# Decode attention over compressed blocks in the row layout of the other decode branches, with one sum tile for all three

## The chip, the cores and the metric

One Trainium2 chip, one core. The metric is the device time of one execution in microseconds; the time before is the median of three runs. TensorE (PE) does the matrix products and loads its weights in a queue of its own (PEld); VectorE (DVE) and ScalarE (ACT) do element-wise work and move results out of PSUM; GpSimd (POOL) and SyncE (SP) mainly start transfers.

## The reference, cut to what matters

One layer of a decoder: a prompt of 256 tokens and 8 single decode tokens, each with 2048 cached tokens. Two mixers run on the same normed input, sparse attention and a gated DeltaNet. Their outputs are gated, projected, merged and added to the residual. The change touches only the decode side of the sparse attention. It has three branches for each of 8 sequences: attention over compressed blocks (127 for each sequence, 32 tokens each, made by a small two-layer network), over selected blocks, and over a window of 512. Eight query heads in 2 groups of 4 share 2 key/value heads. The attention weights over the compressed blocks also choose the selected blocks.

```python
kc, vc = compress_finish(jnp.concatenate([pk_past, pk_new], axis=1),
                         jnp.concatenate([pv_past, pv_new], axis=1), cw)   # kc is RMS-normed
o_cmp, p_cmp = cmp_attend(q, kc, vc, qpos, slopes)                         # scores - slope * distance
idx, valid = select_blocks(p_cmp, qpos, kc.shape[1], -(-(past_len + DS) // SEL_BLOCK))
o_slc = slc_sample(q, kv_slc, cache_slc, page_table, idx, valid, qpos, past_len, slopes)
...
o = g[:, :, 0] * o_cmp + g[:, :, 1] * o_slc + g[:, :, 2] * o_win           # g: sigmoid gates per head
```

## The kernel before

The backbone is a list `halves` of weight pieces. Each piece is loaded by SP into `raw` (three buffers), split into a rounded part `hi` by ScalarE (L332, L409) and a residual `lo` by VectorE (L333, L410), three buffers each, and used by TensorE in three products (`three`, L316) that add up in one of two PSUM banks `acc`. First come the compressions of the 8 sequences' cached keys and then values (`CQ`, 96 products for each sequence, `acc<-hi,w1h` and the like), then the projections of the layer, then the output projections. Between the halves `tick()` advances generators (L253) that trace everything else; `yield n` lets n ticks pass. A scheduler orders the instructions of TensorE, VectorE and ScalarE by priority and by when operands and buffers are free; SP and POOL keep the written order. Tiles of one tag share their buffers: `s8` has 13 large slots, `a` has 5 buffers of up to 264 columns (`NA`, L207), `psb` and `psl` have two PSUM banks each. The input norm `g_xnorm` (L279) runs during the compression of the keys; its sums go over long VectorE reduces (L295) and up to four `a` tiles at once (L300, L301).

The decode attention is in these generators:

- `g_cmp_fin` (L437), for each sequence: activation, the second layer of the network into `kcT` or `vc`, squares `csq` in an `a` buffer, and their sums over 128 channels by two products with a column of ones (L468), copied into `rkc` (L469), whose inverse root is taken once at the end (L472).
- `g_small` (L603): the gates. `gd` holds the compressed branch's gates for 64 query columns, `grow` those of the other two branches by row.
- `g_dec_cmp` (L647): scores as 127 blocks x 64 columns. Each sequence's keys meet all 64 query columns, and `diag` (L641) picks the 4 columns that belong to the sequence. Then a transpose, softmax over 64 rows, a transpose back, the value products with all 64 columns (L680), again `diag`, the gates, and the block scores (`dci`) from which the selection follows.
- `g_dec_slc` (L882) and `g_dec_win` (L812): the other two use a row layout instead. Query columns sit in a tile `qm` with zeros, `qk` (L787) makes four 32-column products side by side, one for each pair of group and sequence parity, and softmax runs over 128 rows of which 64 are used. Values go through `pv_part` (L801) into `po`, and `pv_take` (L808) copies them by ScalarE into a tile `X` for each branch.
- at the end of `g_dec_win` (L870) a gather `smo` adds both `X` tiles (2 x 8 products of 8 columns) and the new token's part to `oD`; after it `g_oa` (L1579) frees `oA`, and `g_gdn` starts with `dec` (L1140).

Of the kernel before, what the change touches and what calls it, by code (L numbers as in the profile page):

```python
# [20 lines left out]
NB = 8  # L21
# [34 lines left out]
def shape_constants():  # L56
# [19 lines left out]
    sl64 = np.broadcast_to(slope.reshape(2, 1, 4), (2, NB, 4)).reshape(64)  # L76
    c.add("cmpb", -(PAST - kendd)[:, None] * sl64[None])
# [67 lines left out]
def program(tc, A):  # L145
# [26 lines left out]
    def psb(name):  # L172
        return ps_s.tile([128, 512], F32, tag="ps", name=name)
# [55 lines left out]
    rkc = cp.tile([128, 16], F32, name="rkc")  # L229
# [9 lines left out]
    gd = cp.tile([128, 64], F32, name="gd")  # L239
    grow = cp.tile([128, 2], F32, name="grow")  # L240
# [196 lines left out]
    def g_cmp_fin(kv, b, ps, n):  # L437
# [10 lines left out]
        if kv == 0:  # L448
# [9 lines left out]
            p3 = psb("cf")  # L458
            if b is None:
                for g in range(2):  # L460
                    mm(p3[:, 16 * g:16 * g + 15], ones, sq[:, g, :nn])
# [39 lines left out]
    def g_qstat(h):  # L501
# [7 lines left out]
        if h == 7:  # L509
# [19 lines left out]
            qx = slot("qm", [128, 640])  # L529
            G.memset(qx, 0.0)  # L530
# [72 lines left out]
    def g_small(ps):  # L603
# [24 lines left out]
        mm(p2[:, 0:64], ones[0:24, :], x[:, 0:2].rearrange("p a b r -> p (a b r)"))  # L628
        S.activation(gd, p2[:, 0:64], AF.Copy)
        xp = tp.tile([24, 2, 2, 2, 32], F32, name="gxp", tag="a", bufs=NA)  # L630
        V.memset(xp, 0.0)
        for br in range(2):
            for c in range(2):
                V.tensor_copy(xp[:, br, c, :, 0:16].rearrange("p g (i r) -> p g i r", r=4),
                              x[:, 2 + 2 * br:4 + 2 * br].rearrange("p a (i c) r -> p c a i r", c=2)[:, c])
            mm(p2[:, 192 + br:193 + br], xp[:, br].rearrange("p c g x -> p (c g x)"), ones[0:24, 0:1])
        V.tensor_copy(grow, p2[:, 192:194])
        V.tensor_scalar(beh, smt[:, :, 64:72], 0.5, None, ALU.mult)
        mark("small")

# [1101 lines left out]
```

## Time and profile before

| | |
|---|---|
| median of three runs | 1137.02 us (1135.52 to 1137.14) |
| the profiled execution | 1137.88 us, span 1136.2 us |
| mean granted TensorE clock | 0.994 |
| TensorE busy | 1112.4 us, 98% |
| VectorE busy | 697.1 us, 61% |
| ScalarE busy | 572.7 us, 50% |
| DMA | 222.17 MB, mean 196 GB/s |

The page's chain of work that ended last is 92% TensorE. A timeline row gives start, duration, engine, line, operation, output tile <- inputs, shape and count; a merged row covers all its instructions, and in brackets stands the idle time before it with its cause. A matmul on 32-bit floats shows as two instructions. Durations of matmuls overlap, so the distance between two starts tells more than a duration does.

### The profile page before, as it was taken

The numbers are of one execution on the slowest core, as the hardware profiler recorded it, in microseconds if no ns is written. First come the engines' busy times: TensorE is split into PE (matmuls) and PEld (weight loads), VectorE is DVE, ScalarE is ACT, GpSimd is POOL, SyncE is SP. The second block draws the span as 40 slices with busy tenths as digits, with TensorE's granted clock in tenths as the row PEclk, the third lists the DMA queues.
The fourth block names the chain that finished last, engine by engine and source line by source line (L and its number), as shares of the span: only waits on it lengthen the run. The fifth ranks groups of instructions, "written<-read, shape, count | busy, mean of one in ns | idle before, by whom it ended". The sixth has DMA issues, their size and how long they took to land.

```text
span 1136.2 us, 25323 instructions
## 1 busy us (share of the span) xinstructions
PE 1112.4 (98%) x9558; PEld 1069.3 (94%) x9558; DVE 697.1 (61%) x1523; ACT 572.7 (50%) x1138; POOL 144.2 (13%) x227
## 2 busy tenths in 40 slices
PE   4999999999999999999999999999999999999998
PEld 3989999999999987897989999999999999999998
DVE  3578565443657776783566577677547575487443
ACT  4445655444634766673454465545344554444332
POOL 4430244200001310113022100102000000000000
PEclk9989999999999999999999899999999999999999
DMA  9873676435445784568998755657454355556663
GB/s 302 255 241 124 202 205 203 152 95 160 161 138 177 218 214 135 159 196 220 281 390 291 268 174 176 201 179 220 138 187 148 119 165 177 181 184 223 201 236 125
DMA packets 77069, 222.17 MB, mean 196 GB/s; under 512 B 10625, under 2 KB 27850, under 8 KB 75410
## 3 DMA queue, kind: packets, MB, share of 16 engines
q1 hardware_dynamic: 59346, 164.36, 44.7%
q0 software_dynamic: 15008, 44.98, 13.8%
q10 hardware_dynamic: 2592, 11.21, 2.6%
q8 instruction: 75, 1.23, 0.4%
q14 instruction: 48, 0.39, 0.1%
HBM read 202.90 MB, written 17.60 MB: 194 GB/s over the span
## 4 chain that ended last, share of the span: by engine, by line
PE 92%; DVE 1%; ACT 0%; issue 0%; ACTq 0%
PE acc L205 77%; PE inv L205 1%; PE po L205 1%; PE gtr L202 1%; PE pvo L205 1%; PE ps L205 1%; PE gsc L205 1%; PE cf L205 1%; PE kk L205 1%; PE vnb L202 1%; PE uw L205 1%; DVE xt L306 1%; PE pst L202 0%; PE og L205 0%; PE wsc L205 0%; PE kvtr L202 0%
## 5 line engine op out<-in xcount | busy, mean ns | idle before, releaser
L333 DVE TENSOR_TENSOR lo<-raw,hi 128x1024 fp32r<-128x1024 f32 (+1 forms) x250 | 304.8, 1220 | 212.5 <-ACT hi L332 206.1
L205 PE MATMUL acc<-xh,hi 128*128 128x264 f32 (+1 forms) x1488 | 433.8, 292 | 0.0
L332 ACT ACTIVATE hi<-raw 128x1024 fp32r<-128x1024 f32 (+1 forms) x250 | 263.9, 1056 | 329.7 <-PE acc L205 269.0
L205 PE MATMUL acc<-xl,hi 128*128 128x264 f32 (+1 forms) x1488 | 426.9, 287 | 0.5 <-issue 0.5
L205 PE MATMUL acc<-xh,lo 128*128 128x264 f32 (+1 forms) x1488 | 426.3, 287 | 0.0
L205 PEld LDWEIGHTS acc<-xh,hi 128*128 128x128 f32 (+1 forms) x1488 | 281.0, 189 | 7.6 <-issue 7.0
L205 PEld LDWEIGHTS acc<-xh,lo 128*128 128x128 f32 (+1 forms) x1488 | 280.0, 188 | 2.7 <-issue 2.2
L205 PEld LDWEIGHTS acc<-xl,hi 128*128 128x128 f32 (+1 forms) x1488 | 281.1, 189 | 1.5 <-issue 1.0
L205 PE MATMUL acc<-hi,w1h 128*128 128x254 f32 (+1 forms) x512 | 148.1, 290 | 15.9 <-ACT hi L409 15.9
L205 PE MATMUL acc<-lo,w1h 128*128 128x254 f32 (+1 forms) x512 | 147.4, 288 | 3.4 <-DVE lo L410 3.2
L205 PE MATMUL acc<-hi,w1l 128*128 128x254 f32 (+1 forms) x512 | 145.7, 285 | 0.0
L410 DVE TENSOR_TENSOR lo<-rawc,hi 128x512 fp32r<-128x512 f32 (+2 forms) x136 | 84.0, 656 | 52.5 <-ACT hi L409 48.1
L205 PEld LDWEIGHTS acc<-hi,w1h 128*128 128x128 f32 x512 | 98.4, 192 | 16.0 <-ACT hi L409 15.9
L409 ACT ACTIVATE hi<-rawc 128x512 fp32r<-128x512 f32 (+2 forms) x136 | 74.7, 599 | 62.7 <-PE acc L205 58.0
L205 PEld LDWEIGHTS acc<-lo,w1h 128*128 128x128 f32 x512 | 99.2, 194 | 4.8 <-DVE lo L410 4.5
L205 PEld LDWEIGHTS acc<-hi,w1l 128*128 128x128 f32 x512 | 99.0, 193 | 0.1
L386 POOL DMA_DIRECT2D rawc<-ccmp x125 | 67.3, 538 | 98.2 <-issue 72.3
L205 PE MATMUL acc<-oh,hi 128*128 128x264 f32 x256 | 73.5, 287 | 0.0
L205 PE MATMUL acc<-oh,lo 128*128 128x264 f32 x256 | 72.9, 285 | 0.0
L205 PE MATMUL acc<-ol,hi 128*128 128x264 f32 x256 | 72.7, 284 | 0.0
L205 PE MATMUL acc<-mh,hi 128*128 128x264 f32 x256 | 72.6, 284 | 0.0
L205 PE MATMUL acc<-ml,hi 128*128 128x264 f32 x256 | 72.5, 283 | 0.0
(452 smaller groups left out, 1476.4 us busy)
## 6 DMA issues: line engine op xcount, KB each, us to landing
raw<-win SPq DMA_DIRECT2D x184, 512.0 KB, 3.5
raw<-wpab SPq DMA_DIRECT2D x32, 512.0 KB, 3.9
raw<-wo SPq DMA_DIRECT2D x32, 512.0 KB, 4.3
rawc<-ccmp SPq DMA_DIRECT2D x126, 128.0 KB, 2.7
rawc<-ccmp POOLq DMA_DIRECT2D x125, 128.0 KB, 3.3
raw<-w SPq DMA_DIRECT2D x8, 512.0 KB, 7.6
wk<-winK SPq DMA_DIRECT2D x8, 512.0 KB, 11.1
o_wk<-wk POOLq DMA_DIRECT2D x8, 512.0 KB, 9.0
```

What stands on the lines that cost most here:

```text
L202: T.transpose(out, in_, ident[0:n, 0:n])
L205: T.matmul(out, lhsT, rhs, start=start, stop=stop, **k)
L306: V.scalar_tensor_tensor(xt[i][:, k, :], xt[i][:, k, :], P("nw")[:, kk:kk + 1], rx, ALU.mult, ALU.mult)
L332: S.activation(self.hi, self.raw, AF.Copy)
L333: V.tensor_sub(self.lo, self.raw, self.hi)
L386: e.dma_start(rawc[kv, b][j // 8][:, j % 8].rearrange("p s c g -> p (s c g)"), src[kv, bass.ds(r, 1)].rearrange("o d f -> (o d) f"))
L409: S.activation(h, src, AF.Copy)
L410: V.tensor_sub(l, src, h)
```

## The change

The compressed branch takes the row layout: `qk` makes the scores as 128 rows x 127 blocks, and the softmax runs on them in place. The inverse key norms are needed by row, so the squares of two sequences are summed by four 32-column products with a 0/1 matrix `four` into a PSUM tile `css` that lives from sequence 1 to 7; an even sequence's `csq` waits for the odd one. The weights are transposed once ungated (for the block scores, read from PSUM) and once gated, and the value products are 32-column tiles over key rows 0 to 63 and 64 to 126. Their result is copied into one tile `X`, which lies in the slot of `qm`; the other two branches add theirs by VectorE. The gather reads one `X`. `g_small` makes three row gates. `diag`, `gd`, `rkc` and the two old `X` slots go.

```diff
-    c.add("cmpb", -(PAST - kendd)[:, None] * sl64[None])
+    c.add("kd", np.broadcast_to(-(PAST - kendd)[None], (128, NCMP)))
+    c.add("four", np.broadcast_to((np.arange(60) // 4 == 7)[None], (128, 60)))
...
+            elif b % 2 == 0:
+                L["csq"] = sq
             else:
-                for g in range(2):
-                    mm(p3[0:127, g:g + 1], sq[:, g, :], ones[:, 0:1])
-                V.tensor_copy(rkc.rearrange("p (g b) -> p g b", g=2)[0:127, :, b], p3[0:127, 0:2])
-                if b == NB - 1:
-                    rk = tp.tile([128, 16], F32, name="rk2", tag="rk2")
-                    rsq(rk[0:127], rkc[0:127], 1.0 / 128, 4 * EPS, [127, 16])
-                    V.tensor_scalar(rkc[0:127], rk[0:127], SCALE, None, ALU.mult)
+                if b == 1:
+                    L["css"] = psl("css")
+                i, sqs = b // 2, (L.pop("csq"), sq)
+                for j in range(4):
+                    mm(L["css"][32 * j:32 * j + 32, 0:127], C("four")[:, 28 - 4 * i:60 - 4 * i], sqs[j // 2][:, j % 2, :],
+                       start=i == 0, stop=i == 3)
+                if i == 3:
+                    rsq(rkr, L.pop("css")[:, 0:127], 1.0 / 128, 4 * EPS, [128, 127])
+                    V.tensor_scalar(rkr, rkr, SCALE, None, ALU.mult)
...
-            qx = slot("qm", [128, 640])
-            G.memset(qx, 0.0)
+            qx = slot("qm", [128, 1664])
+            G.memset(qx[:, 0:640], 0.0)
+            L["X"] = qx[:, 640:1664].rearrange("p (b d) -> p b d", b=NB)
...
-        mm(p2[:, 0:64], ones[0:24, :], x[:, 0:2].rearrange("p a b r -> p (a b r)"))
-        S.activation(gd, p2[:, 0:64], AF.Copy)
...
-        for br in range(2):
+        for br in range(3):
+            xp = tp.tile([24, 2, 2, 32], F32, name="gxp", tag="a", bufs=NA)
+            V.memset(xp, 0.0)
...
+            mm(p2[:, br:br + 1], xp.rearrange("p c g x -> p (c g x)"), ones[0:24, 0:1])
...
-        for g in range(2):
-            pt = psb("dcs")
-            for b in range(NB):
-                mm(pt[0:127, 64 * b:64 * b + 64], L["kcT"][:, b, g, :], qf)
-            for o, pv, w in diag(pt[0:127], SCm[0:127], g):
-                V.tensor_tensor(o, pv, rkc[0:127, 8 * g + w.start:8 * g + w.stop, None].to_broadcast([127, w.stop - w.start, 4]),
-                                ALU.mult)
-        V.tensor_add(SCm[0:127], SCm[0:127], C("cmpb", 127))
+        SC = tp.tile([128, 127], F32, name="dcs", tag="a", bufs=NA)
+        PT = tp.tile([128, 128], F32, name="dcp", tag="a", bufs=NA)
+        m1 = tp.tile([128, 4], F32, name="dcm", tag="dcm")
+        pt = psb("dcs")
+        for i in range(4):
+            qk(pt, i, lambda c, g: L["kcT"][:, 2 * i + c, g, :])
+        V.tensor_mul(SC, pt[:, 0:127], rkr)
+        V.scalar_tensor_tensor(SC, C("kd"), C("c64")[:, 1:2], SC, ALU.mult, ALU.add)
...
         yield 5
-        p2 = psb("dct")
-        tr(p2[0:64, 0:127], SCm[0:127, :])
...
         p3 = psb("dct")
-        tr(p3[0:127, 0:64], E[:, 0:127])
-        V.tensor_copy(PT[0:127], p3[0:127, 0:64])
+        tr(p3[0:127, 0:128], SC)
...
+        V.tensor_scalar(SC, SC, grow[:, 0:1], None, ALU.mult)
         yield 3
-        for g in range(2):
-            p5 = psb("dcv")
-            for b in range(NB):
-                mm(p5[:, 64 * b:64 * b + 64], L["vc"][0:127, b, g, :], PT[0:127, :])
-            for (o, pv, _), (_, gv, _) in zip(diag(p5, oD, g), diag(p5, oD, g)):
-                V.tensor_copy(o, pv)
-        V.tensor_mul(oD, oD, gd)
+        tr(p3[0:127, 128:256], SC)
+        S.activation(PT[0:127], p3[0:127, 128:256], AF.Copy)
...
+        yield 2
+        for b in range(NB):
+            if b % 4 == 0:
+                po = PV("pvo")
+            for g in range(2):
+                for t, rows in enumerate((slice(0, 64), slice(64, 127))):
+                    j, c, o = 2 * g + t, 2 * (b % 2) + g, 128 * (b % 4)
+                    mm(po[32 * j:32 * j + 32, o:o + 128], PT[rows, 32 * c:32 * c + 32], L["vc"][rows, b, g, :])
+            if b % 4 == 3:
+                S.activation(L["X"][:, b - 3:b + 1, :], po.rearrange("p (b d) -> p b d", b=4), AF.Copy)
...
-    def pv_take(po, w, b):
+    def pv_take(po, b):
         if b % 4 == 3:
-            S.activation(L["X", w][:, b - 3:b + 1, :], po.rearrange("p (b d) -> p b d", b=4), AF.Copy)
+            x = L["X"][:, b - 3:b + 1, :]
+            V.tensor_add(x, x, po.rearrange("p (b d) -> p b d", b=4))
...
-        for w in range(2):
-            for b in range(NB):
-                mm(o[:, :, b, :], L["X", w][:, b, :], gx[:, :, b, :], start=False, stop=w * b == 7)
-        V.tensor_add(oD, oD, pt[:, 0:64])
-        del L["X", 0], L["X", 1]
+        for b in range(NB):
+            mm(o[:, :, b, :], L["X"][:, b, :], gx[:, :, b, :], start=False, stop=b == 7)
+        V.tensor_copy(oD, pt[:, 0:64])
```

## Rows read from the trace of the kernel before

**Rows 1.** Busy times of the page: us, share of the span, instructions.

```profile
PE 1112.4 (98%) x9558; PEld 1069.3 (94%) x9558; DVE 697.1 (61%) x1523; ACT 572.7 (50%) x1138; POOL 144.2 (13%) x227
```

**Rows 2.** What TensorE waited for: us in total, times, longest us.

```profile
PE acc L205 <- ACT hi L409: 15.9, 1, 15.9
PE acc L205 <- DVE lo L410: 3.2, 2, 2.6
```

**Rows 3.** Stretches of 20 us: busy us of each engine, clock, DMA share, GB/s.

```profile
60.00:80.00 20.00, 17.44 (x121) 16.99 (x120) 15.43 (x18) 9.34 (x16) 6.98 (x13) 0.83 0.83 256
80.00:100.00 20.00, 19.90 (x166) 19.45 (x166) 19.32 (x39) 13.34 (x21) 1.07 (x2) 1.00 0.15 40
```

**Rows 4.** TensorE's timeline around one isolated sum of squares (start, duration).

```profile
142.92 0.50 PE L205 MATMUL cf<-cst,csq 128*127 128x1 f32 x4
143.28 0.38 PE L205 MATMUL acc<-lo,w1h 128*128 128x286 f32 x1
143.50 0.29 PE L205 MATMUL acc<-hi,w1l 128*128 128x286 f32 x1
143.62 0.30 PE L205 MATMUL acc<-hi,w1h 128*128 128x286 f32 x1
```

**Rows 5.** TensorE's timeline at the first of the two groups of scores.

```profile
315.21 1.88 PE L205 MATMUL dcs<-qd,kcT 128*127 128x64 f32 x16
316.90 0.36 PE L205 MATMUL acc<-xh,lo 128*128 128x264 f32 x1
```

**Rows 6.** TensorE's timeline at the value products of the compressed branch.

```profile
334.53 3.68 PE L205 MATMUL dcv<-dcp,vc 127*128 127x64 f32 x32
338.02 0.37 PE L205 MATMUL acc<-xl,hi 128*128 128x264 f32 x1
```

**Rows 7.** TensorE's timeline at the gather and what follows it.

```profile
630.90 1.46 PE L205 MATMUL smo<-cst,X 128*128 128x8 f32 x12
632.21 0.42 PE L202 MATMUL cvt<-cst,qkvr 128*128 128x128 f32 x2
632.47 2.30 PE L205 MATMUL smo<-cst,X 128*128 128x8 f32 x20
634.62 1.36 PE L205 MATMUL dec<-smt,cst 128*128 128x8 f32 x8
635.83 0.57 PE L205 MATMUL acc<-xh,hi 128*128 128x264 f32 x1
```

**Rows 8.** Two stretches after the gather, columns as in rows 3.

```profile
634.00:635.90 1.90, 1.90 (x16) 1.90 (x15) 0.19 (x1) 0.00 (x0) 0.00 (x0) 0.80 1.04 433
635.90:641.90 6.00, 6.00 (x28) 6.00 (x28) 1.90 (x7) 1.49 (x3) 0.00 (x0) 0.50 0.99 335
```

**Rows 9.** TensorE's timeline at 32-column products of the DeltaNet's decode.

```profile
660.86 1.08 PE L205 MATMUL sw<-sst,wq 128*32 128x128 f32 x32
661.87 0.39 PE L205 MATMUL acc<-xl,hi 128*128 128x264 f32 x1
662.10 0.28 PE L205 MATMUL acc<-xh,lo 128*128 128x264 f32 x1
```

**Rows 10.** TensorE's timeline at products in tiles of 32 rows and columns.

```profile
812.62 0.44 PE L205 MATMUL inv<-P,prod 32*32 32x16 f32 x32
812.99 1.10 PE L205 MATMUL inv<-U,At 128*128 128x64 f32 x8
```

**Rows 11.** VectorE's timeline between 60 and 92 us.

```profile
60.87 0.16 DVE L469 COPY rkc<-cf 127x2 f32<-127x2 f32 x1 [1.21 <-PE cf L205]
...
71.27 1.26 DVE L410 TENSOR_TENSOR lo<-rawc,hi 128x512 fp32r<-128x512 f32 x2
...
91.26 0.43 DVE L444 SCALAR_TENSOR_TENSOR chs<-ct,cy 128x254 f32<-128x254 f32 x1
```

**Rows 12.** ScalarE's timeline: the squares of the third sequence.

```profile
68.11 0.36 ACT L456 ACTIVATE csq<-cf 128x254 f32<-128x254 f32 x1
```

More of the change, by code (lines that the diff above doesn't have):

```diff
@@ L228, in program @@
     hb = cp.tile([128, 2], F32, name="hb")
-    rkc = cp.tile([128, 16], F32, name="rkc")
+    rkr = cp.tile([128, NCMP], F32, name="rkr")
     kcTp = cp.tile([128, 2, 15], F32, name="kcTp")
@@ L238, in program @@
     smt = cp.tile([128, 2, 72], F32, name="smt")
-    gd = cp.tile([128, 64], F32, name="gd")
-    grow = cp.tile([128, 2], F32, name="grow")
+    grow = cp.tile([128, 3], F32, name="grow")
     acc2 = cp.tile([128, 128], F32, name="acc2")
@@ L457, in g_cmp_fin @@
             yield 8
-            p3 = psb("cf")
             if b is None:
+                p3 = psb("cf")
                 for g in range(2):
@@ L627, in g_small @@
         p2 = psb("gdp")
[L628 to L632 removed]
+        for br in range(3):
+            xp = tp.tile([24, 2, 2, 32], F32, name="gxp", tag="a", bufs=NA)
+            V.memset(xp, 0.0)
             for c in range(2):
[L634 to L637, printed above, removed]
+                V.tensor_copy(xp[:, c, :, 0:16].rearrange("p g (i r) -> p g i r", r=4),
+                              x[:, 2 * br:2 * br + 2].rearrange("p a (i c) r -> p c a i r", c=2)[:, c])
+            mm(p2[:, br:br + 1], xp.rearrange("p c g x -> p (c g x)"), ones[0:24, 0:1])
+        V.tensor_copy(grow, p2[:, 0:3])
         V.tensor_scalar(beh, smt[:, :, 64:72], 0.5, None, ALU.mult)
         mark("small")
[L641 to L644 removed]
     def g_dec_cmp():
@@ L671, in g_dec_cmp @@
+        V.reciprocal(m1[:, 2:3], m1[:, 1:2])
+        V.tensor_scalar(SC, SC, m1[:, 2:3], None, ALU.mult)
+        yield 5
         p3 = psb("dct")
-        tr(p3[0:127, 0:64], E[:, 0:127])
-        V.tensor_copy(PT[0:127], p3[0:127, 0:64])
+        tr(p3[0:127, 0:128], SC)
         PR = tp.tile([128, 16], F32, name="dpr", tag="dpr")
-        V.tensor_reduce(PR[0:127], PT[0:127].rearrange("p (c r) -> p c r", r=4), AX.X, ALU.add)
-        yield 3
-        for g in range(2):
-            p5 = psb("dcv")
-            for b in range(NB):
-                mm(p5[:, 64 * b:64 * b + 64], L["vc"][0:127, b, g, :], PT[0:127, :])
-            for (o, pv, _), (_, gv, _) in zip(diag(p5, oD, g), diag(p5, oD, g)):
-                V.tensor_copy(o, pv)
@@ L683, in g_dec_cmp @@
-        V.tensor_mul(oD, oD, gd)
+        for c in range(2):
+            V.tensor_reduce(PR[0:127].rearrange("p (g i c) -> p c g i", g=2, c=2)[:, c],
+                            p3[0:127, 64 * c:64 * c + 64].rearrange("p (g x) -> p g x", g=2)[:, :, 0:16]
+                            .rearrange("p g (i r) -> p g i r", r=4), AX.X, ALU.add)
+        V.tensor_scalar(SC, SC, grow[:, 0:1], None, ALU.mult)
+        yield 3
+        tr(p3[0:127, 128:256], SC)
+        S.activation(PT[0:127], p3[0:127, 128:256], AF.Copy)
@@ L773, in row_softmax @@
         V.reciprocal(sn[:, 3:4], sn[:, 3:4])
-        V.tensor_mul(sn[:, 3:4], sn[:, 3:4], grow[:, w:w + 1])
+        V.tensor_mul(sn[:, 3:4], sn[:, 3:4], grow[:, w + 1:w + 2])
         V.tensor_mul(sn[:, 4:5], sn[:, 4:5], sn[:, 3:4])
@@ L1580, in g_oa @@
         yield from wait("attn")
-        yield from wait("oD", 2)
+        yield from wait("oD")
         for g in range(2):
```

23 lines of the change are left out of this document (4 added, 19 removed).

## The prediction

> **What bounds the kernel now.** I read the page's busy times first. TensorE is busy for 1112.4 of 1136.2 us, VectorE for 61% of the span [rows 1]. Next comes the list of what TensorE waited for. One wait of 15.9 us for the first cache pages lies at the start, waits for the residual split (`lo`, VectorE) come to 3.2 us, and nearly nothing else is there [rows 2]. So the time is the sum of what TensorE has in its queue, and an instruction taken out of that queue is worth its start-to-start spacing. It isn't worth its listed duration, because matmuls overlap: in the plain stream one `acc` matmul starts 0.12 us after the other and lists 0.29 [rows 4]. Everything below is counted in spacings. [...] Around 70 us TensorE waits for VectorE, and its clock is low for part of that stretch (0.83 over 60 to 80 us) [rows 2, 3]. [...]
>
> **What is removed, all on the path.** (1) The squares of the compressed keys are summed by two matmuls with one moving column for each of 8 sequences, and each shows as two instructions. An isolated group of four starts at 142.92, `acc` goes on at 143.28, and the first `acc` after it takes 0.22 instead of 0.12 to its successor [rows 4]: 0.36 + 0.10 = 0.46 us. Eight groups: 3.7 us. (2) The scores of all 64 query columns against every sequence's keys: two groups of 16 instructions, 1.69 us from the first to the next `acc` [rows 5], with some 0.1 for the change over: 2 x 1.75 = 3.5 us. (3) The value products, 32 instructions from 334.53 to 338.02 [rows 6], with the change over 3.6 us. (4) Half of the final gather, because there is one sum tile instead of two: 12 instructions took 1.31 us and 20 took 2.15 [rows 7], that is 0.108 each; 16 of them are 1.7 us. Together 12.5 us.
>
> **What is added.** The replacement for (1) to (3) uses weights of 32 columns, so four products lie side by side in the array. The trace has just this form: 32 instructions `sw`, 128 rows by 32 columns with 128 moving columns, from 660.86 to 661.87, 0.0316 us each, and the next `acc` is 0.10 late [rows 9]. I count 0.10 ahead of a group as well, so 0.20 for each group. Key squares: now once for two sequences, 4 groups of 8, each 8 x 0.0316 + 0.20 = 0.45, together 1.8 us. Scores: 32 x 0.0316 + 0.20 = 1.2 us. Value products: 64 instructions, since each key range is cut into rows 0 to 63 and 64 to 126; 64 x 0.0316 + 0.20 = 2.2 us. Together 5.2 us. Bounds: the shortest row of tiles that differ in rows and columns is `inv`, 32 instructions in 0.37 us [rows 10], 0.012 each, though with 16 moving columns; with that for the value products and with no change over for the squares, 3.1 us. At the other end short groups may not overlap (0.09 for each instruction of the squares, from rows 4: 2.9 + 0.8 us) and the value products may take twice the spacing (4.2): 9.1 us. I take 5.2, because `sw` has the same shape.
>
> [...] In rows 10, tiles on different rows write one PSUM tile at 0.012 us each, so they do overlap. [...]
>
> **Edits that I cost at nothing on the path.** The gate tile now gets three columns by 3 matmuls (6 instructions) where 1 + 2 stood (6 as well). The two transposes stay two. VectorE loses 8 copies of two columns and gets a reciprocal root over 127 columns instead of 16, 12 operations and a scaling: each is under the 0.63 us that a 512-column subtraction costs [rows 11], so at most 8 us spread around 160 us. VectorE has the room there; TensorE shows no wait after 80 us except some tenths [rows 2]. The four sum-tile adds move from ScalarE to VectorE, again about 0.63 us each, four in 90 us. What is queued behind such an add is the next `lo`; three `raw`, `hi` and `lo` buffers stand between it and TensorE. If that cover were gone, each add would cost its 0.63 us, 2.5 us together. No DMA and no work on the SP or POOL queue is moved past another, except that the constants grow by 123 columns (63 KB) and that two 8 KB slots fewer are taken late in the kernel, which can only let loads go earlier.
>
> **What is not passed on.** The first two groups of squares lie ahead of the wait at 70 us, which ends when `lo` does [rows 11]. What TensorE saves before (0.46 x 2 - 0.45 = 0.5 us) only lets it wait longer. VectorE loses one copy there that had waited 1.21 us for TensorE [rows 11]; at most 1.4 us could come back, but the long reduce behind the copy hangs on ScalarE too, and I count 0.2. That leaves 0.3 us to take off.
>
> **The sum.** 12.5 - 5.2 - 0.3 = 7.0 us. The profiled execution took 1137.88 us (span 1136.2), so it would take 1130.9; the median of the three runs is 0.9 below it, 1137.0, and with that the forecast is 1130.0 us. With the two bounds of the added work: 3.1 to 9.1 us, that is 1134 to 1128.
>
> **The rivals.** *The clock stays up.* From 630.7 to 635.8 TensorE runs only matmuls of 8 columns (two `cvt` of 128 between them), and in this stretch the clock falls: the last 8 take 1.21 instead of 0.86 us and the next 28 `acc` take 6.0 instead of 3.4 [rows 7, 8]. That is 3.0 us. The change cuts the stretch to about 3.4 us. For a clock that stays: the value products, 3.5 us of 64-column matmuls, passed with the clock at full [rows 6]. Against: around 70 us a wait of only 2.6 us was enough for a fall [rows 2, 3], and 8 columns are nearer to a wait than to 64. The time would be 1127. [...]
>
> *Buffers run short, and it ends slower.* The squares of an even sequence now stay in one of the five `a` buffers until the odd one is done. Those written at 68.11 [rows 12] would stay until about 96 us, while the input norm keeps up to four `a` tiles between 78 and 96 us and the next sequence needs three; `chs` at 91.26 [rows 11] then comes some 6 us later, and the evacuation of an accumulator may wait too. It happens where VectorE is busy for 19.3 of 20 us [rows 3]. The accumulators have two banks, so it costs nothing until the delay is longer than one sequence's 96 matmuls, 11.5 us; beyond that TensorE stands still for each further microsecond, and a stop of over 2 us brings a half-clock stretch of about 3 us as at 70 us. For a result slower than before the stops must come to over 7 us. Two such stops of 4 us with 3 us of low clock each give 14 - 7, about 1144. Against it: the tiles of the norm are gone by 97 us, and so is the shortage.
>
> *The tiles don't pack.* If 32-column products start at 0.11 us like the ones they replace, 128 instructions cost 14.1 us, with change overs 15.3, where 10.8 are taken away, and the 1.7 of the gather is all that stands against it: 1139.8. Rows 9 speak against it for just this shape.
>
> *The wait at 70 us goes too.* If the order on VectorE shifts so that `lo` comes ahead of the long reduce, 2.6 us and the low clock behind it (about 3 us) come back: 1124.
>
> **How the numbers follow.** Forecast 0.52; clock stays up 0.25; buffers run short 0.09, about half of it with no more than a loss of part of the gain; tiles don't pack 0.05; the wait goes 0.09. Likeliest: 1130.0 us. The range reaches down past the clock case, to 1125.5, and up to the upper bound of the added work, 1134.5; outside lie the wait that goes (0.09), the tiles that don't pack and most of the shortage, less than 0.2. About 0.2% (2.3 us) is what a measurement of this kernel can tell from no change. Faster: forecast, clock, wait and part of the shortage, less the tail above 1134.7, 0.86. Same: 0.08, from the shortage and the upper bound. Slower: 0.06.
>
> **What would show it.** In the changed profile: 32 score instructions in about 1 us, 64 value instructions in about 2 us and contiguous, 16 gather instructions in 1.7 us, groups of 8 squares in 0.25 us; TensorE's busy time lower by about 7 us with its idle time as before, and the clock near 630 us either at half for some 7 us again (forecast) or at full. Wrong would be: value products at 0.06 or more, a new wait of TensorE for an `acc` bank or for `lo` between 80 and 170 us, or a TensorE that is idle for more than 26 us.

## The result and the profile after

The change makes the kernel slower. In six runs each it takes 1144.37 us (median; 1142.61 to 1147.28) where the kernel before takes 1135.78 (1134.74 to 1137.14): ratio 1.0075, 95% interval 1.0059 to 1.0091. The forecast was 1130.0 with a range of 1125.5 to 1134.5. The profiled execution took 1142.61 us (span 1140.7, mean granted clock 0.992). It is the fastest of the six, and the kernel before was profiled above its median (1137.88 us), so the two traces lie 4.7 us apart and not 8.6.

TensorE's work shrank, by less than the 7 us of the forecast. This is the busy line of the page after, which answers to [rows 1]:

```profile
PE 1107.1 (97%) x9574; PEld 1062.2 (93%) x9574; DVE 699.8 (61%) x1516; ACT 573.5 (50%) x1136; POOL 145.6 (13%) x227
```

TensorE is busy 5.3 us less and the span is 4.5 us longer, so its idle time grew by 9.8 us. The list of what it waited for, kernel after (us in total, times, longest), which answers to [rows 2], says where:

```profile
PE acc L205 <- ACT hi L408: 15.8, 2, 14.5
PE pvo L205 <- DMA wv<-winV: 3.2, 3, 1.8
PE acc L205 <- DVE lo L409: 3.0, 2, 1.9
PE pvo L205 <- DMA gv<-cslv,idx: 2.3, 1, 2.3
PE rrow L202 <- DVE aT L1176: 1.5, 1, 1.5
PE dq L205 <- DVE dkq L1414: 1.4, 1, 1.4
PE kk L205 <- DVE edl L1162: 1.0, 1, 1.0
PE uw L205 <- ACT wT L1292: 0.7, 1, 0.7
PE kk L205 <- DVE l L1158: 0.7, 1, 0.7
PE acc L205 <- ACT gate L1498: 0.6, 1, 0.6
```

The first and third line are old. The others are new, and none of them names an instruction that the change wrote: selected values (`gv`), window values (`wv`), the DeltaNet's chain (`rrow`, `kk`, `dq`), a gate. But for `uw` (at 884 us) they fall in four stretches (kernel after; busy us of PE, PEld, DVE, ACT, POOL with their counts, clock, DMA share, GB/s):

```profile
540.00:550.00 10.00, 7.73 (x73) 7.12 (x72) 1.53 (x4) 1.69 (x2) 0.00 (x0) 0.83 1.03 287
600.00:620.00 20.00, 16.83 (x176) 15.06 (x174) 10.80 (x17) 8.43 (x17) 4.51 (x8) 0.95 0.90 336
640.00:660.00 20.00, 17.96 (x152) 16.58 (x152) 14.86 (x42) 13.73 (x33) 0.00 (x0) 0.91 0.42 138
700.00:710.00 10.00, 6.90 (x64) 5.77 (x56) 7.40 (x25) 8.58 (x28) 0.00 (x0) 0.84 0.52 179
```

Each of them has idle time and a mean clock under 1. The trace's clock record has the granted clock at 0.50 for 3.4 us from 546.5, 6.8 us from 618.1, 3.4 us from 648.8 and 3.4 us from 706.9 us. Two of these begin within a wait, the others 0.7 and 1.4 us behind the end of one. At 0.50 one `acc` starts 0.22 us after the other, at 1.00 it is 0.12. So a wait with such a stretch behind it costs its own length, and then about half the length of the stretch.

The changed parts themselves, on TensorE's timeline of the kernel after (start, duration, instructions): a quarter of a group of squares (two of its eight instructions), the scores, the value products, the gather. They answer to [rows 4 to 7].

```profile
143.30 0.29 PE L205 MATMUL acc<-hi,w1l 128*128 128x286 f32 x1
143.52 0.41 PE L205 MATMUL css<-csq,cst 128*32 128x127 f32 x2
143.85 0.52 PE L205 MATMUL acc<-hi,w1h 128*128 128x286 f32 x2
...
312.59 1.08 PE L205 MATMUL dcs<-kcT,qm 128*32 128x127 f32 x32
313.60 0.39 PE L205 MATMUL acc<-xh,lo 128*128 128x264 f32 x1
...
334.61 1.95 PE L205 MATMUL pvo<-vc,dcp 64*32 64x128 f32 x64
336.49 0.39 PE L205 MATMUL acc<-xh,hi 128*128 128x264 f32 x1
...
633.14 1.90 PE L205 MATMUL smo<-cst,qm 128*128 128x8 f32 x16
634.90 1.04 PE L205 MATMUL dec<-smt,cst 128*128 128x8 f32 x8
635.79 0.37 PE L205 MATMUL acc<-xh,hi 128*128 128x264 f32 x1
```

The scores take 1.01 us from first to next `acc`, the value products 1.88 (0.029 each), the 16 gather instructions 1.76 (0.11 each). Behind the gather, where the kernel before ran at half clock [rows 8], the kernel after has:

```profile
632.00:634.90 2.90, 2.90 (x29) 2.90 (x27) 0.95 (x1) 1.38 (x3) 0.00 (x0) 1.00 0.86 218
634.90:641.90 7.00, 7.00 (x61) 7.00 (x61) 4.50 (x15) 2.35 (x6) 0.00 (x0) 1.00 0.69 227
```

To place gain and loss I compare the start of the same dense product (the n-th `acc` matmul; their order is the same in all kernels) in two traces. The table gives that difference to the kernel before, at times of the kernel before, less its value at 195 us. That point is taken because kernels whose first 300 us are the same instructions still differ by up to 4.5 us by then. Negative is ahead. It is one execution each, so tenths mean little, but steps of 2 us can be placed.

| kernel | 500 | 590 | 627 | 669 | 706 | end |
|---|---|---|---|---|---|---|
| after | -6.9 | -4.0 | +0.9 | +0.7 | +7.8 | +6.4 |
| one_sum | 0.0 | -0.7 | +4.3 | +6.0 | +15.0 | +11.7 |
| hold_to_gather | -6.9 | -5.1 | -7.2 | -7.2 | -0.3 | -1.2 |
| late_state | -6.9 | -5.3 | -6.6 | -7.9 | +0.1 | -1.3 |
| two_sums | -6.8 | -4.4 | -6.5 | -7.3 | +0.2 | -1.1 |
| pair | 0.0 | -0.6 | +3.2 | +2.8 | +3.7 | +2.7 |
| two_sums_ticks | -5.0 | -5.2 | -5.2 | -5.1 | -5.1 | -5.1 |
| one_sum_held | -4.9 | -5.3 | -5.4 | -3.4 | +5.3 | +2.1 |
| one_sum_free | -4.9 | -5.8 | -2.1 | -2.0 | +7.2 | +3.9 |
| one_sum_held_tight | -5.0 | -4.9 | -5.0 | -3.1 | -2.6 | -2.7 |

The kernel after is 6.9 us ahead at 500 us. That is the forecast's figure, but some 2 us of it are work that was only put off: with the pauses of before (two_sums_ticks, explained below) the lead there is 5.0. Between 540 and 710 us the kernel after gives all of it back, and at the end it is 6.4 us behind. The experiments ask what stands behind these 200 us.

### The profile page after: what moved, and what is told of

Read it like the earlier page. It is cut to its first block, busy times and chain, and to the rows that moved or that the text cites. A ratio compares the mean times of both kernels' runs of the same rounds, so it can differ in the third digit from the quotient of the medians.

```text
span 1140.7 us, 25329 instructions
## 1 busy us (share of the span) xinstructions
PE 1107.1 (97%) x9574; PEld 1062.2 (93%) x9574; DVE 699.8 (61%) x1516; ACT 573.5 (50%) x1136; POOL 145.6 (13%) x227
## 4 chain that ended last, share of the span: by engine, by line
PE 89%; DMA 4%; issue 3%; ACT 1%; POOLq 1%; POOL 1%; DVE 1%; SPq 0%; ACTq 0%
PE acc L205 75%; DMA gv<-cslv,idx 2%; PE inv L205 1%; PE po L205 1%; PE gtr L202 1%; DMA wv<-winV 1%; PE ps L205 1%; DMA rawc<-ccmp 1%; PE pvo L205 1%; POOLq L384 1%; PE gsc L205 1%; PE cf L205 1%; POOL rawc L385 1%; PE vnb L202 1%; PE uw L205 1%
```

## The experiments

Two kinds of theory were open. *Order and buffers*: one sum tile means that large buffers (the 13 slots of `s8`) come free earlier, so that later tiles take other buffers and wait for other things. *The work itself*: the adds on VectorE, or the row layout, cost more than counted. Each kernel's runs have their own runs of the kernel before beside them; the medians of those lay between 1135.25 and 1136.35 us. Of each edit the main lines are shown.

**The step "one sum tile" alone (one_sum).** The kernel before, old layout, with one tile for the two sums in the slot of `qm`, the second added by VectorE, and a gather of 8 products.

```diff
-            S.activation(L["X", w][:, b - 3:b + 1, :], po.rearrange("p (b d) -> p b d", b=4), AF.Copy)
+            x = L["X"][:, b - 3:b + 1, :]
+            if w:
+                V.tensor_add(x, x, po.rearrange("p (b d) -> p b d", b=4))
+            else:
+                S.activation(x, po.rearrange("p (b d) -> p b d", b=4), AF.Copy)
```

> The kernel before with one part of the change alone: one sum tile in the slot of qm for the selected and the window branch (copy, then add by VectorE), one gather of 8 products; scores, squares and values of the compressed branch as before. TensorE has 1.7 us less to do. Theory 'buffers': the same bunched loads, so waits of pvo for gv and wv appear here too, and the time is 1138 to 1148 although no other part of the change is in. Theory 'order': anything from 1130 to 1145. Theory 'adds': the two adds alone cost little, 1134 to 1137.

Measured: 1146.12 us, ratio 1.0092 (1.0067 to 1.0117). This step alone, with nothing of the row layout, costs as much as the whole change (the intervals overlap). So the loss doesn't need the row layout.

**Holding the freed buffers, first try (hold_both, hold_slc, hold_win).** The kernel after with one or two spare tiles in the places where the kernel before took buffers for its sum tiles.

```diff
         P_ = pt_rows("sP", sc, 8, 120)
+        L["D", 0] = slot("D0", [128, 16])
+        V.memset(L["D", 0][:, 0:1], 0.0)
...
         V.tensor_copy(oD, pt[:, 0:64])
+        V.tensor_copy(L["D", 0][:, 1:2], L["D", 0][:, 0:1])
```

> The changed kernel with two empty large buffers taken where the two X tiles stood and kept until the gather is done; nothing else differs. Theory 'buffers' (the two freed buffers let value gathers and state loads start early, they bunch, and the value products meet late data): the waits of pvo for gv and wv are gone, idle after 500 us under 2 us, time 1127 to 1131. Theory 'order' (any edit deals the scheduled order of the DeltaNet start anew, and the waits of dq, kk and rrow for VectorE come with it): about 1138 to 1144. Theory 'adds' (the sum-tile adds on VectorE hold up the work behind them): 1142 or more, since the adds stay.

> Only the first of the two empty buffers, taken from the value products of the selected branch until the gather. Theory 'buffers': the bunched gathers at 515 to 529 us and the wait for gv (2.3 us and a low clock behind it, about 4 us) go; if the state load near 607 us needs the second buffer, the waits for wv (3.2 us and a low clock, about 6 us) stay: 1136 to 1141; if one buffer is enough for both, 1128 to 1132. Theories 'order' and 'adds': 1140 or more.

> Only the second empty buffer, taken from the value products of the window branch until the gather. Theory 'buffers': the wait for gv stays (about 4 us with its low clock), the state load comes after 620 us again and the waits for wv go: 1132 to 1137. Theories 'order' and 'adds': 1140 or more.

Measured: 1142.52 (1.0066, 1.0044 to 1.0089), 1140.44 (1.0042, 1.0027 to 1.0056) and 1142.32 us (1.0062, 1.0041 to 1.0084). These three decide nothing. The spare tile's last copy depends on nothing that comes late, so the scheduler ran it at once (in the traces the copies start within 0.5 us of the memsets, at 500.9 and 589.3 us), and the buffers were free again. The first state load was still issued at 606.5 to 607.3 us. Why hold_slc lies below the kernel after by more than the intervals isn't known.

**Holding them to the gather (hold_to_gather).** Now the spare tiles are first written from the value products and last from the gather's result, so that the data keep them alive.

```diff
+            S.activation(L["D", w][:, 32 * (b // 4):32 * (b // 4) + 32], po[:, 0:32], AF.Copy)
             x = L["X"][:, b - 3:b + 1, :]
             V.tensor_add(x, x, po.rearrange("p (b d) -> p b d", b=4))
...
         V.tensor_copy(oD, pt[:, 0:64])
+        for w in range(2):
+            V.tensor_copy(L["D", w][:, 64:128], pt[:, 0:64])
```

> The kernel after with two spare tiles that take the large buffers of the two sum tiles of before: each is first written from the value products (32 columns, ScalarE) where before wrote its sum tile, and last written from the gather's result, so both buffers stay taken from the sums to the gather, while the four adds stay on VectorE. Theory 'buffers' (with one sum tile a large buffer comes free earlier, so that the first 1 MB state load of the DeltaNet decode is issued at 607 instead of 624 us, into the last window value loads): the first state load is issued at about 624 us again, the TensorE waits for window values (3.2 us in the kernel after) fall to under 1 us, and the time is 1128 to 1133 us. Theory 'adds' (the sums on VectorE hold the work of the next branch up): no change, 1141 to 1146 us. Theory 'row layout' (the new order of the compressed branch itself): no change, 1141 to 1146 us.

Measured: 1137.41 us, ratio 1.0011 (0.9995 to 1.0027), between the ranges that the theories gave. Extra work made the kernel 7 us faster. The order of loads shows why. These are the issues of the first state loads (1 MB each, on ScalarE's queue): kernel before,

```profile
624.47 0.35 ACTq L1370 DMA_DIRECT2D sst<-stS  x1
627.99 0.34 ACTq L1370 DMA_DIRECT2D sst<-stS  x1
```

kernel after,

```profile
607.57 0.35 ACTq L1364 DMA_DIRECT2D sst<-stS  x1
631.13 0.34 ACTq L1364 DMA_DIRECT2D sst<-stS  x1
```

and hold_to_gather:

```profile
626.07 0.35 ACTq L1370 DMA_DIRECT2D sst<-stS  x1
631.37 0.37 ACTq L1370 DMA_DIRECT2D sst<-stS  x1
```

In the kernel after the first one goes out 17 us earlier, between the last window value loads (issued at 605.3, 607.1 and 608.5 us). With the buffer held it goes out behind them, and TensorE doesn't wait for `wv` at all. The last `wv` load of the kernel after lands 16.7 us after its issue; in two_sums and vector_copies below, where the first state load goes out behind these loads and TensorE doesn't wait for them, the last one takes 14.8 and 14.3. How full the stretch is doesn't decide it: the DMA share of 600 to 620 us is 0.90 in the kernel after and 0.95 in two_sums. The stretch 590 to 627 us, in which the kernel after loses 4.9 us, now gains 2.1. The stretch 669 to 706 us loses 6.9 us, as in the kernel after (7.1), so the buffers held here aren't the whole cause.

**The same from the other side (pair).** The kernel before, with its two sum tiles as the halves of one buffer; no add, no new layout.

```diff
-        L["X", 0] = slot("X0", [128, NB, 128])
+        xx = slot("X0", [128, 2, NB, 128])
+        L["X", 0], L["X", 1] = xx[:, 0], xx[:, 1]
```

> The kernel before, with one edit: its two sum tiles are the two halves of one large buffer, so the second takes no buffer of its own; same copies on ScalarE, same gather of 16, same compressed branch. 'Buffers': the first state load is issued at about 607 us, TensorE waits about 2 to 4 us for the window values, and the time is 1139 to 1146 us. 'Adds' and 'row layout': as before, 1134 to 1138 us.

Measured: 1139.11 us, ratio 1.0034 (1.0021 to 1.0048). One buffer fewer costs 3.5 us without any change in the work. Its waits that the kernel before doesn't have (pair, all of TensorE):

```profile
PE pvo L205 <- DMA wv<-winV: 3.7, 2, 2.4
```

The first state load goes out at 610.4 us, the last `wv` load at 610.7. The loss lies at 608 to 627 us only. Near 700 us nothing is lost.

**State loads later (late_state).** The kernel after, with the first two state loads five planner steps (calls of `tick()`) later.

```diff
-        state(0)
-        state(2)
...
         yield 5
+        state(0)
+        state(2)
```

> The kernel after, with the first two state loads moved in the program to five planner steps later (behind the decode convolution's vector work); nothing else. 'Buffers', through the collision of the first state load with the window values: the loads are issued behind 620 us, the waits for window values are under 1 us and the time is 1130 to 1136 us. If what costs is not the collision but the earlier order of the rest, 1140 to 1146 us.

Measured: 1136.33 us, ratio 1.0004 (0.998 to 1.0027), just above the 1130 to 1136 of the theory; the runs spread widely (1127.9 to 1140.9). The loads go out at 637.9 us. Of the three waits for `wv` one of 2.2 us is left, and the stretch 590 to 627 us gains 1.3 us where the kernel after loses 4.9. So the collision with the state load is the cause of most of that loss, though not of every wait there. The loss near 700 us stays.

**Two sums in two buffers (two_sums).** Row layout; the compressed and the selected sum in one tile, the window's in another as before; a gather of 16.

```diff
+            if w:
+                S.activation(L["X", 1][:, x, :], p, AF.Copy)
+            else:
+                V.tensor_add(L["X", 0][:, x, :], L["X"][:, x, :], p)
```

> The kernel after with the compressed and selected branches summed into a buffer of their own (two adds on VectorE) and the window branch copied to another by ScalarE, as before has them; the gather is 16 products instead of 8. So the row layout is kept and only the saving of buffers is given up. 'Buffers': first state load at about 624 us, 1129 to 1134 us (the gather costs some 1 us more than in the kernel after). 'Adds': half of the adds are left, about 1138 to 1141 us. 'Row layout': 1141 to 1146 us.

Measured: 1134.72 us, ratio 1.0000 (0.9986 to 1.0014), just above the range of 'buffers'. The waits for `wv` are gone. Two losses are left in its trace: the wait for selected values at 544 us (1.8), and 7.5 us between 669 and 706.

**The two added planner steps (two_sums_ticks, after_ticks).** The change also put a `yield 2` into the compressed branch, which sets all that follows back by two planner steps, or 24 dense products. Both kernels take it out again, one from two_sums, one from the kernel after.

```diff
         V.tensor_scalar(SC, SC, grow[:, 0:1], None, ALU.mult)
-        yield 3
+        yield 1
```

> The row layout with two sum tiles (as two_sums), and the pause of three planner steps behind the compressed softmax cut to one, so that all that follows the compressed branch stands at the same dense product as in before (the change had added a pause of two steps). Theory 'order' (the loss of the change is the order of the work behind it, which two things moved: the two extra planner steps and the large buffer that came free; the row layout itself gives what was forecast): no TensorE wait for selected values near 545 us nor for VectorE near 700 us, the lead over before that the row layout has by 500 us (some 7 us) stays to the end, 1126 to 1130 us. Theory 'row layout' (the gain is given back by the branch's own work): as two_sums, 1133 to 1137 us.

> The kernel after with the same cut of the pause from three steps to one; one sum tile, nothing else. 'Order': the wait for selected values near 545 us is gone (some 4 to 5 us back), while the first state load still takes the early buffer (window value waits of 2 to 4 us) and the chain steps bunched at the first gate of the second half, near 700 us, stay: 1137 to 1142 us. If the two planner steps cost nothing: 1142 to 1147 us.

Measured: two_sums_ticks 1132.44 us, ratio 0.9966 (0.9945 to 0.9987); after_ticks 1144.18 us, 1.0079 (1.0056 to 1.0103). So two_sums_ticks beats both kernels, and it is the row layout with two sum tiles and the pauses of before. Its time lies between the ranges of the two theories. These are the waits of 0.3 us or more in its trace for which the kernel before has no line:

```profile
PE kvtr L202 <- ACT dcp L671: 0.5, 1, 0.5
PE acc L205 <- DVE w1l L367: 0.4, 1, 0.4
PE dci L205 <- DVE kn L584: 0.3, 1, 0.3
```

Its lead, 5 us and not the 7 that were expected, stays from 500 us to the end. For the kernel after the expectation failed: the wait at 545 us shrank to some tenths, yet the time is the same. By 500 us the two steps had put off work that came back later, and the loss near 700 us grew. With two tiles the pause makes the difference between a loss near 700 us (two_sums) and none; with one tile the loss is there either way.

**The decode loop tighter (tight_decode).** The kernel after with the pauses in the DeltaNet decode's loop cut from 3 and 4 steps to 2 and 3.

```diff
-                    yield 3
+                    yield 2
...
-                    yield 4
+                    yield 3
```

> The kernel after with the pauses in the DeltaNet decode's loop cut from 3 and 4 planner steps to 2 and 3; nothing else. In the kernel after, the first gate of the second half is written to the buffer of the first decode state and so waits for that state's write-back; dense products have to stop there, and only chain steps run (near 700 us). Theory 'write-back': with the states updated two to four steps earlier the write-back is issued before that gate, the waits rrow 1.5, kk 1.0 and acc 0.6 us and the half-speed stretch near 707 us shrink, and the time falls by 3 to 6 us, to 1138 to 1142 us; the waits near 545 and 615 us stay. If the bunch of chain steps has another cause: 1142 to 1147 us.

What is meant by a bunch is seen on TensorE's timeline of the kernel after (in brackets the idle time before and what ended it):

```profile
699.75 0.85 PE L205 MATMUL sw<-sst,wq 128*32 128x128 f32 x20
700.53 0.43 PE L202 MATMUL rrow<-cst,dec 128*128 128x128 f32 x2
700.89 0.63 PE L205 MATMUL sw<-sst,wq 128*32 128x128 f32 x12
701.46 1.16 PE L205 MATMUL kk<-qkvr 128*128 128x128 f32 x8
704.14 0.41 PE L202 MATMUL rrow<-cst,dec 128*128 128x128 f32 x2 [1.53 <-DVE aT L1176]
705.52 1.13 PE L205 MATMUL kk<-qkvr 128*128 128x128 f32 x8 [0.97 <-DVE edl L1162]
707.25 0.59 PE L205 MATMUL acc<-xh,hi 128*128 128x264 f32 x1 [0.60 <-ACT gate L1498]
```

For 7.5 us no dense product runs. The next dense product waits until an `acc` bank is emptied, and the bank's result is the first slice of the second gate tile, which takes the large buffer of decode state 0. That buffer is free when the state's write-back `o_Ss` has landed. On ScalarE, kernel after (both banks are emptied at once, x2):

```profile
701.92 0.36 ACTq L1457 DMA_DIRECT2D o_Ss<-sst  x1
706.80 0.67 ACT L1498 ACTIVATE gate<-acc 128x264 f32<-128x264 f32 x2
```

The gate comes 4.9 us after the issue. This write-back lands at 706.78 us, 0.02 us before the gate. In the kernel before the issue stands 7.2 us ahead of the gate, and nothing waits:

```profile
688.55 0.36 ACTq L1463 DMA_DIRECT2D o_Ss<-sst  x1
695.70 0.37 ACT L1504 ACTIVATE gate<-acc 128x264 f32<-128x264 f32 x1
```

Measured for tight_decode: 1142.13 us, ratio 1.0056 (1.0039 to 1.0073). The waits on VectorE near 700 us are gone and one of 1.7 us for the gate is left; the write-back is issued at 696.8, the gate written at 704.4. The loss between 669 and 706 us falls from 7.1 to 2.2. Of the time some 2.8 us come back (+5.8 beside +8.6; the intervals overlap). The wait for window values stays (2.2 us); the one for selected values is gone, but near 525 us stand 2.2 us of idle time for which the profile names no cause, with 3.4 us at half clock.

**All repairs with one tile (one_tile_repaired).** The kernel after with late_state, the cut pause and the tighter decode loop together.

> The kernel after, one sum tile kept, with all three repairs: the pause cut to one step, the first two state loads five planner steps later, the decode loop's pauses cut to 2 and 3. Theory 'order': none of the three groups of waits (545, 615 to 619, 700 us) is left above 1 us, 1124 to 1130 us. If the adds on VectorE or the single tile cost something by themselves: 1131 to 1138 us.

Measured: 1134.08 us, ratio 0.9977 (0.9964 to 0.9989). It is some 11 us better than the kernel after and beats the kernel before, but isn't better than two_sums_ticks. The time lies in the range given for adds or a single tile that cost by themselves, not in that of 'order'; but waits are left, of 1.0 us in the selected branch's value products (no cause named), 1.4 for `wv` and 1.0 for the gate, so it doesn't decide between the two.

**The move of the copies alone (vector_copies).** The kernel before with its four copies on VectorE.

```diff
-            S.activation(L["X", w][:, b - 3:b + 1, :], po.rearrange("p (b d) -> p b d", b=4), AF.Copy)
+            V.tensor_copy(L["X", w][:, b - 3:b + 1, :], po.rearrange("p (b d) -> p b d", b=4))
```

> The kernel before with its four copies of the sums (128x512 out of PSUM) moved from ScalarE to VectorE; buffers, gather and compressed branch as in before, and the order of the engines' work all but the same. If the adds on VectorE cost by themselves: 1138 us or more. If only buffers and order cost: 1134 to 1138 us, as before.

Measured: 1135.58 us beside 1135.25, ratio 1.0008 (0.9995 to 1.0022), and its trace runs level with that of the kernel before from 100 us on (within 0.7 us, 0.3 at the end). Four operations of 128x512 on VectorE cost nothing by themselves there; each takes 0.69 us, as long as an add in the kernel after.

**One step from the fastest kernel (one_sum_held, one_sum_free).** Both start from two_sums_ticks and add the window's sum into the same tile, with a gather of 8. one_sum_held keeps the second sum tile's buffer taken by a spare tile up to the gather (the last line of the diff, and a last copy from the gather's result); one_sum_free doesn't and lacks these.

```diff
             if w:
-                S.activation(L["X", 1][:, x, :], p, AF.Copy)
+                V.tensor_add(L["X", 0][:, x, :], L["X", 0][:, x, :], p)
+                S.activation(L["X", 1][:, 32 * (b // 4):32 * (b // 4) + 32], po[:, 0:32], AF.Copy)
```

> two_sums_ticks with the window branch added into the selected branch's sum tile by VectorE and a gather of 8, while a spare tile takes the second sum tile's buffer until the gather. The first state load stays at its place behind the window branch; the decode steps come out bunched at the first gate of the second half. Theory 'two effects' (buffer and bunch): window value waits under 1 us, but the waits on VectorE and the half clock near 700 us, 1135 to 1140 us. If only the buffer costs: 1129 to 1133 us. If the shared tile costs by itself: 1141 us or more.

> The same without the spare tile: the second sum tile's buffer is free, so the first state load takes an earlier one. 'Two effects': in addition the window value waits of 2 to 4 us and the half clock behind them, 1140 to 1146 us. If the buffer costs nothing once the rest is as it is: as one_sum_held.

Measured: one_sum_held 1138.80 us, ratio 1.0034 (1.0020 to 1.0049); one_sum_free 1141.34 us, 1.0059 (1.0041 to 1.0077). Against two_sums_ticks the third sum in the same tile costs some 7.5 us even with the buffer held, and the freed buffer some 2.5 more (the two intervals overlap slightly; the traces differ by 3.3 us at 627). The waits that one_sum_held has and two_sums_ticks doesn't:

```profile
PE acc L205 <- DVE lo L332: 2.1, 1, 2.1
PE kk L205 <- DVE l L1165: 2.0, 1, 2.0
PE kk L205 <- DVE aT L1183: 1.8, 1, 1.8
PE rrow L202 <- DVE aT L1183: 0.7, 1, 0.7
```

one_sum_free has these too (the first 2.7 us long), and 2.2 us for the window values again.

**The bunch taken out (one_sum_held_tight).** one_sum_held with the decode loop's pauses cut as in tight_decode.

> one_sum_held with the pauses in the DeltaNet decode's loop cut from 3 and 4 planner steps to 2 and 3, so that the first state's four updates stand two to four steps earlier. Theory 'gate waits for the state's buffer': the write-back of state 0 is issued some 3 to 5 us before the second gate tile is first written instead of right with it, the waits of TensorE on VectorE (4.5 us in all near 700 us) fall to under 1.5 us, the loss of 10 us between 689 and 706 us halves at least, and the time is 1132 to 1136 us. If the bunch comes from something else: as one_sum_held, 1137 to 1141 us.

Measured: 1133.62 us, ratio 0.9970 (0.9954 to 0.9986). From 1.0034 to 0.9970 is 6 to 7 us, for two pauses. The stretch 700 to 710 us, first one_sum_held, then this kernel:

```profile
700.00:710.00 10.00, 8.22 (x50) 7.95 (x51) 3.65 (x13) 4.46 (x13) 3.27 (x6) 0.68 0.52 182
```

```profile
700.00:710.00 10.00, 8.99 (x73) 8.80 (x74) 5.44 (x12) 8.35 (x24) 0.00 (x0) 1.00 0.31 102
```

and its write-back and gate, 6.9 us apart instead of 5.2:

```profile
694.74 0.36 ACTq L1464 DMA_DIRECT2D o_Ss<-sst  x1
...
701.61 0.65 ACT L1505 ACTIVATE gate<-acc 128x264 f32<-128x264 f32 x2
```

The loss of 8.7 us between 669 and 706 falls to 0.5. With that the second cause is shown too: dense products stop at the second gate tile until a large buffer is free. Counted in dense products (`acc` matmuls from the start), the write-back goes out at the 4320th in the kernel before, pair, vector_copies and two_sums_ticks, which lose nothing here. In the eleven other kernels with the loop as it was, the products stop at the 4416th until the write-back is through. What is left here is 1.0 us for the gate and the wait of 2.1 us for `lo`. The tighter loop wasn't run in a kernel without the bunch, so a small gain of its own isn't excluded.

## Why the prediction was wrong, point by point

The steps from the kernel before to the kernel after, each less its own runs of the kernel before:

| step | kernel | us | ratio |
|---|---|---|---|
| row layout, planner steps as before | two_sums_ticks | -3.9 | 0.9966 (0.9945 to 0.9987) |
| the window's sum into the same tile, buffer held | one_sum_held | +3.6 | 1.0034 (1.0020 to 1.0049) |
| that buffer released | one_sum_free | +6.1 | 1.0059 (1.0041 to 1.0077) |
| the sums in the slot of `qm`, second buffer released | after_ticks | +7.8 | 1.0079 (1.0056 to 1.0103) |
| two planner steps more | after | +8.6 | 1.0075 (1.0059 to 1.0091) |

The second step stands clear of the first by more than the intervals. The third is 2.5 us, with intervals that overlap slightly, and the last two, 1.7 and 0.8 us, can't be told from nothing.

The shares hang on the order in which the steps are taken. By way of two_sums (-0.9) and hold_to_gather (+1.8) the planner steps come first and cost 3.0 us, the third sum in the tile 2.7, and the two freed buffers 6.8; only the last is clear of the intervals. Either the planner steps or the shared tile is enough to bring the loss near 700 us, and it is paid once.

- **The step that failed** is the paragraph on edits costed at nothing: it took the order of the work behind the changed branch as given. Two of its terms cost most. The first is the sentence on slots: two slots fewer "can only let loads go earlier". Loads did go earlier, and that was the harm. The first state load went into a stretch where the DMA engines are 90% busy (600 to 620 us above), ahead of window values that TensorE needs sooner (pair: 3.5 us with nothing else changed; 6.8 us from hold_to_gather to the kernel after). The prediction had asked only whether a load comes too late, never which other load it is put in front of.
- **The four adds** are the second, costed at nothing with a loss of 2.5 us if their cover went. As work that is right (vector_copies). But the shared tile changed the scheduler's order of the DeltaNet decode, state 0's write-back came too late for the second gate tile, and that cost 6 to 7 us (one_sum_held against one_sum_held_tight, 1.0034 and 0.9970). The prediction knew that the scheduler orders by buffers and operands, and still took the order behind the change as given. Why the scheduler spaces the state's updates out when the third sum shares the tile isn't settled. Neither the engine (vector_copies) nor the buffer (one_sum_held) does it alone, and with two planner steps more the bunch is there with two tiles too (two_sums).
- **The two planner steps** were missed: the step from `yield 3` to `yield 3` and `yield 2` stands in the diff and has no term. In the kernel after it is worth nothing that can be measured; with two sum tiles it costs some 3 us (two_sums against two_sums_ticks, intervals that just touch). It brings the wait for selected values at 545 us, though: with it ten gathers are issued back to back from 515.7 us and the slowest lands after 22.2 us, where the kernel before spreads them (the slower of the two landings that its trace has there takes 11.8).
- **The accounting of TensorE** was right in kind. Measured like the terms of the sum, with the change over at both ends, the scores cost 1.2 us as taken, the value products 2.1 where 2.2 was taken, and the gather 0.11 for each instruction, as taken. Twice the spacing for the value products (4.2 us), which the upper bound of the added work counts, is shown by no run; the trace has 0.029 us for each, not 0.06. Only the squares were mis-sized. Before, a group costs 0.45 us, 3.6 in all, as taken. After, the scheduler runs an even sequence's products as soon as its squares are there, so three of the four groups come in pieces. There are eight pieces, and each costs 0.5 to 0.6 us, whether it has 2, 4 or 8 instructions: about 4.3 instead of 1.8. The squares cost 0.6 us more than before where 1.9 was to be saved. Scores, values and squares then give 2.3 + 1.5 - 0.6 = 3.2, less 0.9 us of new short waits near 328 us (`kvtr`, `dci`) 2.3. two_sums_ticks measures 3.9 with an interval from 1.5 to 6.2, so the time bears this out only roughly. Its trace leads by 5.1 us; 2.4 of that is in products that the change doesn't touch (`po`, `gsc`, `ps`), and why they take less there isn't known.
- **The clock rival came true** (chance 0.25). With the gather of 8 products the clock behind it stays up in the kernel after (1.00 from 632 to 641.9 us) and in 9 of the 12 other kernels that have it; 3 show 3.4 us at half. With the gather of 16 it falls in all five, for 3.4 us once and 6.8 four times. What it gave was outweighed: the kernel after has 17.1 us at 0.50 in its four stretches of new waits, beside 6.8 behind the gather and 6.8 near 72 us in the kernel before.
- **The wait at 70 us** was to stay and grow a little. It shrank from 2.6 to 1.9 us, in all kernels with the row layout. The low clock behind it (0.50 for 6.8 us in the kernel before) isn't tied to that: it is missing in one_sum, pair and vector_copies too, which still wait 2.6 us. **Buffers run short** was a rival for the `a` tiles at 80 to 100 us; that didn't happen. The squares that were to stay from 68 to 96 us are written at 68.50 and summed from 70.67. The right resource class, the wrong pool: it was the large slots 500 us later, by coming free early, not by running short.
- **The tiles pack**, as the forecast had it: 0.032 us for each of the 32 score instructions, 0.029 for each of the 64 of the values.
- Of the signs named in the prediction, "a TensorE that is idle for more than 26 us" is the one that came up: 33.6 us (1140.7 - 1107.1). The chances put 0.06 on slower; no rival had a mechanism behind 540 us.

## What to carry to other kernels

Where one pool of buffers feeds loads, chains and results, a tile that is dropped doesn't just free space: every later tile takes another buffer and inherits another wait. Ask which transfer takes the freed buffer, what it then stands in front of, and which tile now waits for whose write-back. Before such a saving is credited, build the change with the old buffers and pauses kept and drop them in steps of their own; here that separated a gain of 4 us from a loss of 12.

## What the runs showed of the hardware that was not expected

- Waits of TensorE of 1 to 3 us in the midst of dense work were followed or met by 3.4 or 6.8 us at a clock of 0.50 in many places (four of four stretches in the kernel after). Their length doesn't decide it: 2.7 us for `lo` in after_ticks and one_sum_free passed without a fall, 1.4 us for `dkq` in the kernel after, with 0.7 for `l` behind it, was followed by one, and the same 2.6 us for `lo` near 70 us was met by a fall in the kernel before and by none in three other kernels. So the rival that counted on a fall behind each stop of over 2 us isn't borne out. In the traces of the kernels before and after, each fall between 100 us and the end of the work begins within a wait or up to 1.4 us behind one, but for the fall behind the gather of 16 thin products, with no gap [rows 8]. No run shows what brings that one about.
- Products of 32 columns on two row halves into one PSUM tile start as close together as products on 128 rows: 64 of them take 1.88 us in the kernel after (0.029 each), where 32 on 128 rows take 1.01 (0.032 each) [rows 9].
- Executions that are the same up to 300 us lie up to 4.5 us apart by 100 us: a clock of 0.50 for 3.4 or 6.8 us near 28 us or none, with or without another 3.4 or 6.8 near 72 to 76. Single executions are better compared from a later point on.
